# Eight column blocks of an input projection as seven-product units in a two-layer decoder trunk

## The chip, the cores and the metric

The kernel runs on one core of one Trainium2 chip. The metric is the device time of one execution in microseconds. The engines are named as in the profile: PE (TensorE, matrix multiplications), PEld (its weight loads), DVE (VectorE), ACT (ScalarE), POOL (GpSimd) and SP (SyncE, which here only issues loads and stores). Each engine works through its instructions in the order in which they stand in the compiled program, and waits where an instruction needs a result of another engine.

## What is computed

Two identical layers over 512 positions of width 1024, all in 32-bit floats. In each layer four token mixers share one input projection `w_in`, and the branches are gated, projected up, added and projected out; a SwiGLU follows:

```python
def mixer_block(h, cos, sin, w_in, ...):
    u = h @ w_in                       # h = rms_norm(x, ln1)
    (fq, fk, fv, ff, gq, gk, gv, glr, gr, rq, rk, rv, rg, z, xbc, dt, gates) = split_cols(u, IN_SPLITS)
    y_a = forgetting_attention(...)    # fox: softmax over fq, fk, fv with forget gates ff
    y_b = gated linear attention       # gla: gq, gk, gv, glr; its output is gated by silu(gr)
    y_c = retention                    # ret: rq, rk, rv with rotary positions; gated by silu(rg)
    xbc = silu(causal_depthwise_conv(xbc, conv_w, conv_b))
    y_d = ssd_chunked(...)             # ssd: xbc and dt; gated by silu(z)
    g = sigmoid(gates)                 # 4 branches x 1024 columns
    merged = sum over b of g[b] * (y_b @ w_up_b)
    return merged @ w_out
x = x + mixer_block(rms_norm(x, ln1)); x = x + swiglu(rms_norm(x, ln2))
```

The conv has four taps over 768 channels (six tiles of 128). z has 512 columns, gq and gk 256 each.

## The kernel before, in words

**Layout.** Activations stand with features on the 128 partitions and the 512 positions along the row, so a width of 1024 is eight tiles (`KD = 8`). Weights are the stationary operand, in blocks of 128 x 128; eight blocks in the order of use make a slab of 512 KB, which SP loads (L250, tile `wr`).

**Precision.** A 32-bit number is split in a high part that PE takes at its faster 32-bit rate and a rest: `split` (L211) is a cast on ACT (L212) and a subtraction on DVE (L213). A product of two split numbers is three matmuls (`mm3`, L200: high x high, high x low, low x high), all issued by `mm` (L198). So each slab costs ACT a cast of 128x1024 (`wh`) and DVE a subtraction of 128x1024 (`wl`), two slabs ahead of their use (`ahead`, `AHEAD = 2`). The activations are split as well: `xh` is x times the norm's gain, cast on ACT, and `xl` the rest on DVE (`feed`, L392 to 397); the norm's factor per position is multiplied in after the projection, since it is only known later (`rstd`).

**Projections.** `group` (L426) takes four column blocks with the eight tiles of x in the outer loop, so that PE can begin with the first tile; PE needs a slab of weights for every two tiles. `proj` (L435) takes one block of 128 columns: 24 matmuls of 512 columns. A layer begins with a group of four blocks of the conv's input (C_X), two more by `proj`, then the four blocks of z; the conv of tile i (L476: one multiplication and three multiply-adds on DVE, a silu on ACT) is issued beside them. In layer 0 the positions' sines follow (`rotary`, L352), then the wide projection (gv, glr, dt and the forget gates).

**Mixers and fill.** `ssd`, `gla`, `ret` and `fox` are generators that yield between their steps; `drain` (L462) pulls work off a list `fill` at every yield, by its estimated microseconds. The fill holds the projections that are not needed yet (gq, gk, gr, rg, rq, rk, rv, fq, fk, fv), the gates (`gate_quad(b, q)`, L1146: four projections and one sigmoid over 128x2048) and the up-projections (`up_of(b, q)`: four columns blocks, multiplied by the gates and added to `merged`). The compiler's scheduler then orders each engine's instructions by its own estimate of when they can run, so the source does not show the final order alone; the orders in this document are the compiled ones.

**Fox.** For each of four heads and four blocks of 128 queries: scores by two matmuls; an addition of the forget sums on DVE (L1063), the causal mask on POOL (L1064), the row maximum on DVE (L1066), the exponential with its row sum on ACT (`act`, L236), its reciprocal and a scaling on DVE (L1069, L1070). PE transposes the result (L1079), it is split (ACT cast, DVE subtraction), and PE multiplies it with the values. `finish` (L1094, L1095) adds the two halves of a head's output and splits the tile; only then can `up_of(0, .)` use it. After fox the fill still holds the second four gates of branch 0, `mix(gate_quad(0, 1), up_of(0, 0))`, and `up_of(0, 1)`.

**Tables of ACT.** Silu and sine, exponential and logarithm, and sigmoid lie in three sets of functions; `act` (L227) issues a table load (L231) where the set changes. Copies and casts do not ask for one.

**Seven products.** The FFN's first projection already runs most of its column blocks by a scheme of Strassen's kind: a unit of four column blocks by eight row blocks is seen as two by two quarters, each of four row blocks and two column blocks, and the positions are halved to 256. Seven products of quarter sums replace eight. Of the activations, four sums of halves are needed (t1 to t4, made once by `sums`: scaled copies of x on ACT, subtractions on DVE, and a split). Of the weights, the quarters are loaded apart (tiles `rq`, and one `wr`), added and subtracted on DVE and split; three low parts are made by a negated copy on ACT and a load on POOL's queue that adds the weights to it. Results are added from three PSUM banks with copies on ACT (128x256) and additions on DVE.

**Order and buffers.** `wp` holds two raw slabs `wr` and three each of `wh` and `wl`. The mixers' scratch is a pool of 33 tiles of 128x512 (`tp`) and two of 128x2048 for gates (`gp`).

## Time and profile before

| | |
|---|---|
| median of three runs | 1717.66 us (1717.35 to 1718.27) |
| the profiled execution | 1718.72 us, its span 1717.0 us |
| granted clock of TensorE, mean | 0.999 |
| PE busy | 1705.9 us, 10140 matmuls |
| ACT table loads | 40 in one group of the trace, 1.28 us each |
| bytes moved by DMA | 195 MB, 114 GB/s |

Views used in the prediction: the *page* with the share of each engine and, in its rows of 40 slices, PEclk, the clock granted to TensorE in tenths (9 is 90% or more); the *waits* of an engine (what it waited for, the total in us, how often, the longest); the *chain* of work that ended last, in order of time (start, duration, engine, line and count of a piece); the *timeline* (start, duration, engine, line, operation, output <- input, partitions x elements, and in brackets the idle time before it and what ended that); *windows* (a stretch, its length, then busy time and number of instructions of PE, PEld, DVE, ACT and POOL, the granted clock, the busy share of the DMA engines, GB/s); and *groups* of like instructions (count | busy us, mean ns of one | idle time before). A row with x2 covers two instructions. Neighbours on an engine overlap a little in their records, so that the distance of two starts is the better price of one.

### The profile page before, as it was taken

What the parts mean: (1) busy time and instruction counts of PE and PEld (TensorE: products, weight loads), DVE (VectorE), ACT (ScalarE), POOL (GpSimd) and SP (SyncE); (2) the same over time, 40 slices, a digit from 0 to 9 for tenths busy, and PEclk for the clock granted to TensorE, in tenths of its full rate; (3) what the DMA queues carried; (4) which work ended last, traced back from release to release, by engine and by line L of the source; (5) the groups of instructions that cost most, each with busy time, mean ns of one, the idle gap of its engine ahead of it and who ended that gap; (6) DMA issues with size and microseconds to landing.
All of it is one profiled execution on the core that took longest, in us unless ns stands there. A gap on an engine that the chain in (4) does not pass through costs nothing.

```text
span 1717.0 us, 25146 instructions
## 1 busy us (share of the span) xinstructions
PE 1705.9 (99%) x10140; PEld 1484.7 (86%) x10140; DVE 1213.2 (71%) x1683; ACT 861.9 (50%) x1190; POOL 225.2 (13%) x227
## 2 busy tenths in 40 slices
PE   8999999999999999999999999999999999999998
PEld 7878888888888999998988788888888889999998
DVE  5867666768677677675777666767776677767666
ACT  5424543546447646464544254435553574655543
POOL 2032110022101010101010322200221010101010
PEclk9999999999999999999999999999999999999999
DMA  5322222222235657575333222222222365665653
GB/s 199 106 74 74 75 82 78 86 86 74 78 112 143 196 134 186 135 186 121 89 99 115 68 74 75 85 76 89 83 86 82 103 172 161 152 175 139 183 108 102
DMA packets 54693, 195.00 MB, mean 114 GB/s; under 512 B 6064, under 2 KB 6448, under 8 KB 54576
## 3 DMA queue, kind: packets, MB, share of 16 engines
q1 hardware_dynamic: 45072, 160.45, 29.2%
q0 software_dynamic: 8640, 31.46, 10.3%
q8 instruction: 79, 1.29, 0.3%
q10 hardware_dynamic: 864, 1.48, 0.2%
q14 instruction: 38, 0.31, 0.1%
HBM read 191.27 MB, written 2.10 MB: 113 GB/s over the span
## 4 chain that ended last, share of the span: by engine, by line
PE 97%; DVE 1%; DMA 1%; ACT 1%; issue 0%; ACTq 0%; DVEq 0%
PE mm L198 65%; PE mx L198 31%; PE mx L1079 0%; DMA x<-in_x_dram 0%; DMA t<-in_ext_dram 0%; ACT wh L212 0%; DVE wl L213 0%; PE mx L679 0%; DVE t L369 0%; ACT L231 0%; DVE t L836 0%; ACT g L236 0%; DVE t L1168 0%; DVE n L407 0%; PE mx L871 0%
## 5 line engine op out<-in xcount | busy, mean ns | idle before, releaser
L212 ACT CAST wh<-wr 128x1024 fp32r<-128x1024 f32 (+1 forms) x240 | 250.0, 1043 | 378.4 <-PE mm L198 238.0
L198 PE MATMUL mm<-xh,wh 128*128 128x512 f32 (+1 forms) x1184 | 429.2, 362 | 0.9 <-DVE t L1168 0.9
L198 PE MATMUL mm<-xh,wl 128*128 128x512 f32 (+1 forms) x1184 | 428.6, 362 | 0.0
L198 PE MATMUL mm<-xl,wh 128*128 128x512 f32 (+1 forms) x1184 | 427.4, 361 | 0.0
L213 DVE TENSOR_TENSOR wl<-wr,wh 128x1024 fp32r<-128x1024 f32 (+1 forms) x220 | 281.8, 1282 | 119.9 <-ACT wh L212 117.6
L198 PEld LDWEIGHTS mm<-xh,wh 128*128 128x128 f32 x1184 | 222.6, 188 | 35.2 <-DVE t L1168 1.8
L198 PEld LDWEIGHTS mm<-xh,wl 128*128 128x128 f32 x1184 | 222.6, 188 | 35.1 <-issue 1.5
L198 PEld LDWEIGHTS mm<-xl,wh 128*128 128x128 f32 x1184 | 222.6, 188 | 33.7 <-issue 1.1
L198 PE MATMUL mm<-t,wh 128*128 128x512 f32 x448 | 140.3, 392 | 0.0
L198 PE MATMUL mx<-xh,wh 128*128 128x256 f32 (+1 forms) x448 | 136.2, 311 | 3.0 <-ACT wh L212 3.0
L198 PE MATMUL mx<-xl,wh 128*128 128x256 f32 (+1 forms) x448 | 138.5, 309 | 0.0
L1287 POOL DMA_DIRECT2D wl<-in_wsq_dram x60 | 51.9, 864 | 518.0 <-ACT wl L1286 337.1
L198 PE MATMUL mx<-f,wh 128*128 128x512 f32 x352 | 108.3, 390 | 0.0
L198 PE MATMUL mm<-f,wh 128*128 128x512 f32 x352 | 106.0, 390 | 0.0
L198 PEld LDWEIGHTS mm<-t,wh 128*128 128x128 f32 x448 | 83.3, 188 | 17.1
L213 DVE TENSOR_TENSOR l<-rq,wh 128x1024 fp32r<-128x1024 f32 x60 | 73.2, 1219 | 33.1 <-ACT wh L212 18.7
L198 PEld LDWEIGHTS mx<-xh,wh 128*128 128x128 f32 x448 | 84.1, 188 | 9.2 <-ACT wh L212 4.0
L198 PE MATMUL mx<-xh,wl 128*128 128x256 f32 (+1 forms) x288 | 91.0, 327 | 0.0
L198 PEld LDWEIGHTS mx<-xl,wh 128*128 128x128 f32 x448 | 84.2, 188 | 5.1
L198 PE MATMUL mm<-t,wl 128*128 128x512 f32 x224 | 87.5, 390 | 0.0
L212 ACT CAST wh<-rq 128x1024 fp32r<-128x1024 f32 x60 | 62.9, 1049 | 43.9 <-PE mm L198 21.5
L198 PEld LDWEIGHTS mm<-f,wh 128*128 128x128 f32 x352 | 66.1, 188 | 13.5
(275 smaller groups left out, 3457.2 us busy)
## 6 DMA issues: line engine op xcount, KB each, us to landing
wr<-in_wst_dram SPq DMA_DIRECT2D x216, 512.0 KB, 3.5
rq<-in_wsq_dram SPq DMA_DIRECT2D x60, 512.0 KB, 5.3
wl<-in_wsq_dram POOLq DMA_DIRECT2D x60, 512.0 KB, 7.1
wr<-in_wsq_dram SPq DMA_DIRECT2D x20, 512.0 KB, 7.3
out_dram<-x SPq DMA_DIRECT2D x8, 256.0 KB, 2.0
x<-in_x_dram SPq DMA_DIRECT2D x3, 512.0 KB, 7.2
wr<-in_wst_dram SPq DMA_DIRECT2D x4, 256.0 KB, 5.6
x<-in_x_dram SPq DMA_DIRECT2D x2, 256.0 KB, 4.5
```

Of the source, the lines that this page charges most:

```text
L198: T.matmul(o, lhsT=l, rhs=r, start=start, stop=stop, skip_group_check=True)
L212: A.copy(out=hi, in_=src)
L213: V.tensor_tensor(out=lo, in0=src, in1=hi.bitcast(F32), op=ALU.subtract)
L1287: G.dma_start(out=lo, in_=wsq[j], accum_op=ALU.add)
```

## The change

Per layer, eight column blocks of `w_in` leave the plain projections: the four of z, and two each of gq and gk. They become two units of the seven-product scheme, which run directly behind the six plain blocks of the conv's input. For that, `sums` and `strassen` move out of the FFN, with the function that finishes a unit as an argument (the FFN calls them as before), and `sums` becomes a generator: in the layer's first group of four blocks, its four sums are issued one at a time at the tiles k = 4, 5, 6 and 7, and the first two negated copies and accumulating loads at k = 6 and 7. At k = 4 in layer 0 the squares and the constants' loads are issued first, as before.

The conv of all six tiles, and in layer 0 `rotary`, move behind the products. One pool `kp` of eight tiles of 128x1024 takes the conv's input, the products' results, the gates and the merged sum; the 128x2048 gate tiles go, and `tp` shrinks from 33 tiles to 24. A sigmoid now covers a pair of gate blocks (128x1024), and a silu of gr and rg one block. The fill is put in another order: `gate_quad(3, 0)` and rv move ahead of ssd, rg behind it, fq and fk into gla, and `gate_quad(0, 1)` into fox; behind fox only `up_of(0, 0)` and `up_of(0, 1)` are left. The table of slabs with wide blocks (`TOKEN`) and the counts of slabs follow. In the changed kernel `mm` is L203, `split` L217 and L218, `act` L241 and its table load L236, fox's transposes L1293.

The diff, cut to what matters:

```diff
-TOKEN = (10, 11, 12, 25, 26, 41, 42)
+TOKEN = (6, 7, 8, 15, 16, 33, 34)
...
-    def mixers():
-        return phase(gp=2, vp=2, bd=1, tp=33)
+    def front():
+        outer = phase(g=64, kp=8)
+        return outer, phase(tq=1, ep=4, rp=5, gl=192, lp=2)
...
-            if hook and k == 4:
-                hook()
+            if hook and k in hook:
+                hook[k]()
...
+    def sums(tb, g, FT):
+        xg = []
+        def scaled(ks):
+            for k in ks:
+                t = FT([P, 2, S])
+                for i in range(2):
+                    act(out=t[:, i], in_=x[:, k + i], func=AF.Copy, scale=g[:, k + i:k + i + 1])
+                xg.append(t)
+        scaled((0, 2))
+        one_, two = slice(0, H), slice(H, S)
+        def make(n, f):
+            t = FT([P, HK, H])
+            for i in range(2):
+                a, b = f(i)
+                V.tensor_tensor(out=t[:, 2 * i:2 * i + 2], in0=a, in1=b, op=ALU.subtract)
+            split(t, *tb[n])
+            return t
+        t1 = make("t1", lambda i: (xg[i][:, :, two], xg[i][:, :, one_]))
+        yield
+        scaled((4, 6))
+        t2 = make("t2", lambda i: (xg[2 + i][:, :, two], t1[:, 2 * i:2 * i + 2]))
+        yield
+        make("t3", lambda i: (xg[2 + i][:, :, two], xg[i][:, :, two]))
+        yield
+        make("t4", lambda i: (xg[2 + i][:, :, one_], t2[:, 2 * i:2 * i + 2]))
...
+        cols = [(C_Z, C_Z + 2 * P), (C_GQ, C_GK)]
+        begin, run = strassen("w_in", l, [tuple(pairs_of(c) for c in u) for u in cols], tb1, KT, True, front_done)
+        steps = sums(tb1, PR("ln1"), KT)
         def first():
-            for k in range(KD):
-                n1.square(k)
-            constants()
-        ps4 = group("w_in", l, [C_X + P * i for i in range(4)], n1, KD, first if l == 0 else None)
+            if l == 0:
+                for k in range(KD):
+                    n1.square(k)
+                constants()
+            next(steps)
+        def third():
+            next(steps)
+            begin(-1)
+        def fourth():
+            next(steps, None)
+            begin(-2)
+        ps4 = group("w_in", l, [C_X + P * i for i in range(4)], n1, KD, {4: first, 5: lambda: next(steps), 6: third, 7: fourth})
         n1.rstd(True)
...
+        run()
+        scope.close()
+        scope = phase(vp=2, bd=1, tp=24)
...
         for i in (4, 5, 0, 1, 2, 3):
-            cin[i] = scaled(ps4[i] if i < 4 else proj("w_in", l, C_X + P * i, n1, KD))
-        conv(4, cin[4])
-        conv(5, cin[5])
-        for i in range(4):
-            sz[i] = scaled(proj("w_in", l, C_Z + P * i, n1, KD))
-            act(out=sz[i], in_=sz[i], func=AF.Silu)
             conv(i, cin[i])
...
-                    if i == 0:
-                        st["t"] = gp.tile([P, 4, S], F32, tag="g", name=nm("g"))
+                    if i % 2 == 0:
+                        st["t"] = KT([P, 2, S])
...
-                    if i == 3:
+                    if i % 2:
                         act(out=st["t"], in_=st["t"], func=AF.Sigmoid)
...
-        fill += [keep(gq, j, C_GQ + P * j, 0.125) for j in range(2)] + [keep(gk, j, C_GK + P * j) for j in range(2)]
-        fill += silus([C_GR, C_GR + P, C_RG, C_RG + P])
+        fill += gate_quad(3, 0) + silus("gr", C_GR, pair_tiles) + tokmajor(rv, C_RV)
         fill += [keep(rq, j, C_RQ + P * j) for j in range(2)] + [keep(rk, j, C_RK + P * j) for j in range(2)]
+        if l == 0:
+            rotary()
         drain(ssd(), PACE[0])
...
-        fill += mix(gate_quad(2, 0), up_of(1, 1)) + mix(gate_quad(2, 1), up_of(2, 0)) + mix(gate_quad(0, 0), up_of(2, 1))
+        fill += mix(gate_quad(2, 0), up_of(1, 1)) + mix(gate_quad(2, 1), up_of(2, 0)) + mix(gate_quad(0, 0), up_of(2, 1)) + gate_quad(0, 1)
         drain(fox(), PACE[3])
-        fill += mix(gate_quad(0, 1), up_of(0, 0)) + up_of(0, 1)
+        fill += up_of(0, 0) + up_of(0, 1)
```

The products of one layer stand in PE's order as (unit, product): (0,1) (0,2) (0,6) (0,5) (0,7) (1,1) (0,3) (0,4) (1,6) (1,5) (1,7) (1,2) (1,3) (1,4). The number of matmuls rises by 4 x (168 - 96) = 288, the number of table loads in ACT's order from 41 to 88.

More of the change, by code (lines that the diff above doesn't have):

```diff
@@ L490, in scaled @@
             return t
[L492 to L506 removed]
+        tb1 = rights(n1, True)
@@ new lines, in layer, with pairs_of, front_done @@
+        cin, gq, gk = [None] * 6, [None] * 2, [None] * 2
+        gates = {}
+        def pairs_of(c):
+            return c, c + P
+        def front_done(u, a, b):
+            both(a, 0.125 if u else None)
+            both(b)
+            if u == 0:
+                for i, t in enumerate((a, b)):
+                    act(out=t, in_=t, func=AF.Silu)
+                    sz[2 * i:2 * i + 2] = t[:, 0], t[:, 1]
+            else:
+                gq[:] = a[:, 0], a[:, 1]
+                gk[:] = b[:, 0], b[:, 1]
@@ L1390, in ready_for @@
         def ready_for(n):
-            m = PLAIN if n == 0 else sum(PARTS[:n])
-            return strassen(list(range(m, sum(PARTS[:n + 1]), 2)))
+            f0 = PLAIN if n == 0 else sum(PARTS[:n])
+            units = [(pairs_of(f * P), pairs_of(FFN + f * P)) for f in range(f0, sum(PARTS[:n + 1]), 2)]
+            return strassen("w_ffn_in", l, units, tb2, FT, False, lambda u, a, b: swiglu(a, b))
         nn = None
@@ L1397, in hook @@
         def hook():
-            sums()
+            for _ in sums(tb2, PR("ln2"), FT):
+                pass
             begin(-2)
-        ps4 = group("w_ffn_in", l, [0, FFN, P, FFN + P], n2, KD, hook)
+        ps4 = group("w_ffn_in", l, [0, FFN, P, FFN + P], n2, KD, {4: hook})
         n2.rstd()
@@ L1413, in layer @@
             end = part == len(PARTS) - 1
-            cap[0] = len(keys) // SLAB + n + (FRONT // SLAB if end and not last else 0)
+            cap[0] = len(keys) // SLAB + n + (6 if end and not last else 0)
             run()
```

380 lines of the change are left out of this document (188 added, 192 removed).

## The prediction

> **What bounds the kernel now.** I read the page first: the engines' shares, then the chain that ended last, then the waits of PE, then timelines of the places that the change touches.
>
> ```profile
> PE 1705.9 (99%) x10140; PEld 1484.7 (86%) x10140; DVE 1213.2 (71%) x1683; ACT 861.9 (50%) x1190; POOL 225.2 (13%) x227
> PE 97%; DVE 1%; DMA 1%; ACT 1%; issue 0%; ACTq 0%; DVEq 0%
> PE mx L198 <- ACT wh L212: 3.0, 3, 1.6
> PE mm L198 <- POOL t L325: 1.4, 1, 1.4
> PE mx L198 <- DVE t L213: 1.2, 2, 0.7
> PE mm L198 <- DVE t L1168: 0.9, 2, 0.5
> PEclk9999999999999999999999999999999999999999
> ```
>
> PE is 97% of the chain and waits 6.5 us in all (the four lines of waits: total, times, longest), at full clock in every slice. So PE work that is removed is time, and so is each new wait of PE: it works in order, and nothing absorbs a gap. Pace, from the chain:
>
> ```profile
> 505.30 21.76 PE mm L198 x96
> 650.71 8.16 PE mm L198 x72
> 860.39 21.77 PE mx L198 x96
> ```
>
> 96 matmuls of N=512 take 21.76 us (0.2267 each; the third row is layer 1's first group), 72 of N=256 inside the FFN's seven products 8.16 us (0.1133 each): products already run without a gap there.
>
> **Part 1, the products.** A unit of four column blocks is 4 x 8 x 3 = 96 matmuls of 0.2267 = 21.76 us before, and 7 x 2 x 4 x 3 = 168 of 0.1133 = 19.04 us after. Four units: 4 x 2.72 = **-10.9 us**, all on the path. A unit loads the same bytes as four slabs did, and three accumulating loads of 512 KB on POOL's queue besides. I price them at nothing:
>
> ```profile
> 26.00:32.00 6.00, 6.00 (x28) 4.98 (x27) 3.06 (x3) 2.11 (x2) 0.00 (x0) 1.00 0.48 172
> ```
>
> Even in the start-up the DMA engines are busy 0.48 of the time by then (the last but one number), and in SP's order the five new loads stand behind those of the first three slabs. If that cover were gone, the fourth slab would come late by what part 2 allows at its upper end.
>
> **Part 2, the start.** ACT is the engine that PE waits for there, and it is nearly gapless:
>
> ```profile
> 13.04 1.12 ACT L212 CAST wh<-wr 128x512 fp32r<-128x512 f32 x2
> 14.56 1.34 ACT L236 ACTIVATE xh<-x,pr 128x512 fp32r<-128x512 f32 x2 [0.40 <-DMA x<-in_x_dram]
> 15.80 1.14 ACT L236 ACTIVATE n<-x 128x512 f32<-128x512 f32 x2
> 16.84 1.32 ACT L236 ACTIVATE xh<-x,pr 128x512 fp32r<-128x512 f32 x2
> 18.90 0.63 ACT L236 ACTIVATE n<-x 128x512 f32<-128x512 f32 x1 [0.73 <-DVE n L407]
> 19.44 1.03 ACT L212 CAST wh<-wr 128x1024 fp32r<-128x1024 f32 x1
> 20.52 0.51 PE L198 MATMUL mx<-xh,wh 128*128 128x512 f32 x1 [1.05 <-ACT wh L212]
> ```
>
> The third slab's cast ends at 20.47 and PE starts on it at 20.52. ACT's order at this place, before (the cast of the third slab is wh_194) and after (wh_207; k_ are scaled copies of x, t1h the split of the first sum):
>
> ```order
> L212 CAST wh_146<-wr_109 128x512 x2
> L236 ACTIVATE xh_134<-x,pr 128x512 x2
> L236 ACTIVATE n_232<-x 128x512
> L236 ACTIVATE n_235<-x 128x512
> L236 ACTIVATE xh_134<-x,pr 128x512 x2
> L236 ACTIVATE n_238<-x 128x512
> L212 CAST wh_194<-wr_114 128x1024
> ```
>
> Up to that cast stood casts and squares alone. After:
>
> ```order
> L241 ACTIVATE k_270<-x,pr 128x512 x2
> L217 CAST wh_153<-wr_115 128x512 x2
> L241 ACTIVATE xh_141<-x,pr 128x512 x2
> L241 ACTIVATE n_245<-x 128x512
> L241 ACTIVATE k_296<-x,pr 128x512 x2
> L241 ACTIVATE n_248<-x 128x512
> L217 CAST t1h_171<-k_273 128x1024
> L241 ACTIVATE xh_141<-x,pr 128x512 x2
> L241 ACTIVATE k_299<-x,pr 128x512 x2
> L217 CAST wh_207<-wr_120 128x1024
> ```
>
> Six k_ copies of these rows and two earlier ones now stand ahead of that cast: 8 x 0.62 (two xh in 1.24, 14.56 to 15.80) + 0.95 for t1h = 5.9 us; one square less (0.5) and the idle 0.40 + 0.73 give some back. **+4.0 us** (3 to 6, the upper end without what is given back).
>
> **Part 3, the entry of layer 1.** The sums add 8 subtractions of 0.6 and 4 of 1.14 (9.4 us) to DVE, under the six plain blocks:
>
> ```profile
> 853.00:876.00 23.00, 23.00 (x103) 19.08 (x102) 22.72 (x30) 15.01 (x21) 5.42 (x3) 1.00 0.32 92
> 854.08 0.68 DVE L1424 TENSOR_TENSOR x<-x,f 128x512 f32<-128x512 f32 x1
> 855.87 1.22 DVE L213 TENSOR_TENSOR wl<-wr,wh 128x1024 fp32r<-128x1024 f32 x1
> 874.51 1.21 DVE L213 TENSOR_TENSOR wl<-wr,wh 128x1024 fp32r<-128x1024 f32 x1
> ```
>
> (The first row's fourth pair is DVE: 22.72 of 23 us; starts of following rows lie 0.6 and 1.14 apart.) DVE came free at 875.7, PE's group of four ends at 882.16 (860.39 + 21.77); by 875.7 + 9.4 = 885.1 it would be done, which makes the fifth slab's subtraction 1 to 3 us late. **+2.0** (0 to 4).
>
> **Part 4, conv.** It lay under the four z projections, which are gone:
>
> ```profile
> L480 DVE SCALAR_TENSOR_TENSOR t<-t,pr,t 128x510 f32<-128x510 f32 x6 | 4.5, 744 | 0.0
> L477 DVE TENSOR_SCALAR t<-t,pr 128x512 f32<-128x512 f32 x6 | 3.1, 537 | 0.0
> ```
>
> 3.1 + 3 x 4.5 = 16.6 us of DVE a layer (three such rows, one for each tap) now stand behind the products, with weight splits queued between them; in layer 0 rotary comes on top. Walking the order with these durations, one weight split is 1 us late and the SSD's first sums another 1.5, less in layer 1. **+2.5** in all (0 to 6). The state's memset, which now stands behind the products on POOL, is needed only in the GLA: nothing. That gates, merged sum and the products' results share eight tiles makes writers wait for older readers, but those readers stand far ahead in the order: nothing, and if not, rival D.
>
> **Part 5, the end of fox.** Here is the largest term. Before, the last softmax and its product ran under projections of the last gates:
>
> ```profile
> 442.54 0.73 DVE L1063 SCALAR_TENSOR_TENSOR t<-mx,cq,t 128x512 f32<-128x512 f32 x1
> 443.95 0.28 POOL L1064 TENSOR_SCALAR_AFFINE_SELECT t<-t 128x128 f32<-128x128 f32 x1
> 444.26 2.33 DVE L213 TENSOR_TENSOR wl<-wr,wh 128x1024 fp32r<-128x1024 f32 x1
> 446.51 0.67 DVE L1066 TENSOR_REDUCE fmx<-t 128x1 f32<-128x512 f32 x1
> 447.21 0.72 ACT L236 ACTIVATE t<-t,fmx 128x512 f32<-128x512 f32 x1 [2.14 <-DVE fmx L1066]
> 448.05 1.28 ACT L231 ACT_TABLE_LOAD   x1
> 450.30 1.91 ACT L236 ACTIVATE g<-g 128x2048 f32<-128x2048 f32 x1
> 448.26 0.49 DVE L1070 TENSOR_SCALAR t<-t,frs 128x512 f32<-128x512 f32 x1
> 452.87 0.97 ACT L212 CAST t<-mx 128x512 fp32r<-128x512 f32 x2 [0.66 <-PE mx L1079]
> 453.49 0.69 DVE L213 TENSOR_TENSOR t<-mx,t 128x512 fp32r<-128x512 f32 x1 [1.83 <-ACT t L212]
> 453.05 4.79 PE mm L198 x21
> 459.70 0.58 ACT L1094 COPY t<-mx 64x512 f32<-64x512 f32 x1 [3.43 <-PE mx L198]
> 460.31 0.68 DVE L1095 TENSOR_TENSOR t<-mx,t 64x512 f32<-64x512 f32 x1 [2.79 <-ACT t L1094]
> 461.03 0.62 ACT L212 CAST t<-t 128x512 fp32r<-128x512 f32 x1 [0.75 <-DVE t L1095]
> 459.66 10.51 PE mm L198 x46
> ```
>
> PE had 4.79 us of projections behind the last transposes and 10.51 us behind the last product. On PE, before (mx_4044 and mx_4067 take the last transposes, mm_4087 is a projection for the gates):
>
> ```order
> L1079 MATMUL mx_4044<-cs,t_3920 128x128
> L1079 MATMUL mx_4044<-cs,t_3989 128x128
> L1079 MATMUL mx_4067<-cs,t_3989 128x128 x2
> L198 MATMUL mm_4087<-xh_134,wl_4020 128x512
> L198 MATMUL mm_4087<-xh_134,wh_4019 128x512
> L198 MATMUL mm_4087<-xl_135,wh_4019 128x512
> ```
>
> The projection goes on behind them. On PE after, at the same place (mx_4504 transposes, mx_4397 the output, mm_4523 the first up-projection of this same output):
>
> ```order
> L1293 MATMUL mx_4504<-cs,t_4446 128x128 x2
> L203 MATMUL mx_4397<-t_4496,t_2796 128x256
> L203 MATMUL mx_4397<-t_4497,t_2796 128x256
> L203 MATMUL mx_4397<-t_4496,t_2799 128x256
> L203 MATMUL mx_4397<-t_4497,t_2799 128x256
> L203 MATMUL mx_4397<-t_4508,t_2802 128x256
> L203 MATMUL mx_4397<-t_4509,t_2802 128x256
> L203 MATMUL mx_4397<-t_4508,t_2805 128x128
> L203 MATMUL mx_4397<-t_4509,t_2805 128x128
> L203 MATMUL mm_4523<-t_4519,wh_4460 128x512
> ```
>
> No projection is left between them. And on ACT, after (t_4446 the last softmax, k_4410 the last pair of gates):
>
> ```order
> L241 ACTIVATE t_4446,frs_4453<-t_4446,fmx_4451 128x512
> L236 ACT_TABLE_LOAD
> L241 ACTIVATE k_4410<-k_4410 128x1024
> L236 ACT_TABLE_LOAD
> L217 CAST t_4496<-mx_4491 128x512
> L217 CAST t_4508<-mx_4504 128x384
> ```
>
> The cast that the output's product waits for stands behind a sigmoid and two table loads, as gates are now taken in pairs. Price in layer 0: exponential to cast is 1.28 + about 1.05 (an estimate: half of 1.91 and a little, for half the columns) + 1.28 + 0.5 (half of the cast pair's 0.97) = 4.1 us; scale and transposes take 2.1 of it beside, so PE waits 2.0. The second split (two subtractions, 0.6 apart) against PE's own work: 0.8. Then copy, add and cast, from 459.70 to 461.03 + 0.62: 2.0, and 0.2 until the copy starts. The last score itself comes 2 late: ACT and DVE are behind from the pair before it, and 20 matmuls (4.5 us) cover a chain of 0.73 + 0.28 (select on POOL) + 0.67 + 0.84 (447.21 to 448.05) + 0.2 + 0.49 = 3.2 that two weight splits of 1.14 are queued among. Sum 7. In layer 1 the order leaves 3 matmuls instead of 8 ahead of those transposes, so 9; one earlier step there, where five copies queue behind a table pair, another 2. **+18** (8, if only the finishing chains and the table pairs show; 24, if weight splits in that chain take 2.33 us, as one did here at 444.26, and not 1.2).
>
> The Trainium skill ("ScalarE: Activation LUTs", section "What ACT_TABLE_LOAD costs") gives 186 ns + 0.833 ns an element for an activation with immediates, so 1.04 us for 128x1024, which no row here shows; by it the sum stays as it is.
>
> **Sum.** -10.9 + 4.0 + 2.0 + 2.5 + 18 = +15.6 on the profiled execution, 1718.72 (span 1717.0 and 1.7 around it), which lies 1.06 above the median 1717.66: 1717.7 + 15.6 = **1733 us**.
>
> **Rivals.** *A, faster:* ACT runs ahead at the end of fox, the gates' pairs are done before the last score, and PE meets finished casts: then the start's 4 us and little else is lost, -10.9 + 4 + 2 = -5, 1713. For it: ACT is only 50% busy. Against: the table loads rise from 41 to 88 in the order, 47 x 1.28 = 60 us more of ACT, and the sequence above is fixed. It decides if less than 5 us of part 5 appear. Chance 0.11. *B, no change:* only the finishing chains (2 x 2.2) and some 4 us of part 5 show beside parts 2 and 3: -10.9 + 4 + 2 + 4.4 + 4 = +3.5 at most, 1715 to 1721; 0.12. *C, the clock:* PE would be mostly idle for 6 to 9 us at two places, and the granted clock could fall behind them. At half the clock for 4 us, about as long as the larger single gaps, each place costs 2 us more: 1737. This trace has no wait longer than 1.6 us and a clock of 1.00 throughout, so it neither shows nor excludes it; 0.12. The Trainium skill ("TensorE: Matmul & The Clock Gate", section "HAM oscillation — how this bites in real kernels") states it so: no idle gap over about 3.4 us, or the array goes back to half its clock. *D, more of the same:* the 47 added table loads also reach PE in the mixers' other steps (8 us, some six loads), 1741; 0.10. My forecast: 0.55.
>
> About 0.2%, 3.4 us, is what a measurement can tell from no change. Faster: A, 0.11. Same: B, 0.12. Slower: the forecast, C and D, 0.77. The range runs from the lower ends (3 + 0 + 0 + 8 - 10.9 = 0, 1718), which leaves out A and half of B, to D with some of the upper ends, 1745.
>
> **What would show it.** The waits of PE should rise from 6.5 to about 33 us, most of them on casts and subtractions of t (L217, L218) at two places, between 460 and 500 us and some 850 us later; PE should start its third slab near 24.5. The FFN's parts should keep their length. If PE's waits stay under 15 us, part 5 is wrong; if a unit of products takes over 20 us, part 1 is.

## The result, and the profile after

| | before | after |
|---|---|---|
| median | 1717.69 us (4 runs) | **1769.72 us** (4 runs, 1767.71 to 1772.70) |
| profiled execution, its span | 1718.72, 1717.0 us | 1772.70, 1770.8 us |
| granted clock, mean | 0.999 | 0.985 |

The ratio is 1.0304 (95%: 1.0286 to 1.0322): 52 us slower. The sign was forecast; the size, +52 against +15.6, lies outside the range. The profiled execution is the slowest of the four and has the lowest clock (0.985; the others 0.987 and 0.988), so that what is counted in its trace is a little more than what the median lost.

The page after: busy shares of the engines, shares of the chain that ended last, the granted clock in 40 slices, and the group of table loads.

```profile
PE 1726.9 (98%) x10428; PEld 1503.6 (85%) x10428; DVE 1250.3 (71%) x1739; ACT 972.5 (55%) x1329; POOL 244.5 (14%) x239
PE 85%; DVE 6%; ACT 5%; issue 3%; DMA 1%; POOL 0%; ACTq 0%; POOLq 0%
PEclk9999999999989999999999999999999899999999
L236 ACT ACT_TABLE_LOAD x80 | 102.6, 1283 | 1.3
```

PE's part of the chain fell from 97% to 85%. Its busy time rose by 21 us, although the change takes work from it: some matmuls are slower. Two slices show a clock below 0.9, and a slice is 44 us. The waits of PE, the largest (total us, times, longest us):

```profile
PE mx L203 <- ACT t L217: 12.1, 5, 3.1
PE mx L203 <- ACT wh L217: 5.4, 5, 2.6
PE mm L203 <- DVE k L1370: 4.4, 4, 1.5
PE mm L203 <- ACT t L217: 4.1, 2, 2.1
```

All waits together are 38.6 us, against 6.5 before. That is 32 more and explains neither +52 nor, with the products' 10.9 taken off, the 63 lost. To see where it goes, two stretches of 20 us of before:

```profile
340.00:360.00 20.00, 20.00 (x94) 16.56 (x93) 15.48 (x26) 11.95 (x16) 4.90 (x5) 1.00 0.34 106
480.00:500.00 20.00, 20.00 (x90) 16.58 (x89) 13.82 (x19) 9.13 (x11) 0.00 (x0) 1.00 0.34 106
```

And the places that lose most after (first pair PE, then PEld, DVE, ACT, POOL, the granted clock):

```profile
340.00:360.00 20.00, 15.23 (x62) 11.36 (x60) 13.97 (x19) 13.27 (x18) 0.00 (x0) 0.97 0.29 90
360.00:380.00 20.00, 18.83 (x70) 14.06 (x70) 17.95 (x29) 14.05 (x20) 5.32 (x4) 0.86 0.09 34
480.00:500.00 20.00, 15.46 (x65) 12.36 (x64) 9.42 (x17) 9.31 (x13) 0.41 (x2) 0.80 0.17 52
900.00:920.00 20.00, 16.70 (x65) 13.02 (x64) 16.32 (x21) 11.45 (x15) 3.01 (x3) 0.83 0.62 172
1220.00:1240.00 20.00, 15.10 (x53) 10.10 (x52) 15.53 (x22) 14.55 (x22) 0.27 (x1) 0.90 0.24 79
1360.00:1380.00 20.00, 13.30 (x56) 10.49 (x55) 10.17 (x17) 10.08 (x15) 1.45 (x2) 0.73 0.16 52
```

Before, PE filled such stretches at clock 1.00. After, 13 to 19 us of 20, at a mean clock down to 0.73. The ends of fox (480, 1360) and the entry of layer 1 (900) were forecast. The first two rows and the fifth, where ret hands over to fox (below: the joint), were not.

A balance adds this up. For each stretch of 20 us I take its length less what the matmuls begun in it take at full pace (0.2267 us for 512 columns, in proportion for fewer, at least 0.057), and subtract the same for the stage in before. "At half pace" is half the time that matmuls took inside stretches of clock 0.50; it is part of the column before it.

| place | forecast | measured, us over before | of that at half pace |
|---|---|---|---|
| products | -10.9 | -10.9 | |
| start, 0 to 60 | +4.0 | +9.2 | 3.6 |
| entry of layer 1, 880 to 960 | +2.0 | +8.7 | 3.2 |
| conv | +2.5 | about 0 | |
| joint of ret and fox, layer 0, 340 to 400 | - | +10.2 | 3.2 |
| the same, layer 1, 1220 to 1260 | - | +9.7 | 2.9 |
| end of fox, layer 0, 480 to 520 | +18 with the next row | +8.7 | 3.6 |
| end of fox, layer 1, and the step before it, 1320 to 1400 | | +14.2 | 3.9 |
| all else | - | +3 | |
| sum | +15.6 | +52.7 (span: +53.8) | 20.4 |

**What half pace is.** PE's timeline at the start, third slab:

```profile
24.43 0.80 PE L203 MATMUL mx<-xh,wh 128*128 128x512 f32 x1 [2.63 <-ACT wh L217]
25.02 0.63 PE L203 MATMUL mx<-xl,wh 128*128 128x512 f32 x1
25.45 0.63 PE L203 MATMUL mx<-xh,wh 128*128 128x512 f32 x1
...
29.32 0.39 PE L203 MATMUL mx<-xh,wl 128*128 128x512 f32 x1
29.55 0.39 PE L203 MATMUL mx<-xh,wh 128*128 128x512 f32 x1
```

And the granted clock (third number from the end) in two half microseconds there:

```profile
24.50:25.00 0.50, 0.50 (x1) 0.43 (x2) 0.50 (x2) 0.50 (x2) 0.00 (x0) 0.50 0.00 0
...
28.00:28.50 0.50, 0.50 (x4) 0.41 (x3) 0.50 (x2) 0.50 (x2) 0.50 (x1) 1.00 0.36 57
```

At the end of a wait of 2.63 us the clock drops to 0.50, at 24.39; starts lie 0.43 us apart instead of 0.23, until 27.81. Seven such drops stand in this trace: at 24.39, 41.46, 358.9, 492.0, 911.9, 1236.1 and 1369.2, for 3.4, 3.4, 6.8, 10.2, 6.8, 6.8 and 13.7 us. All lengths are multiples of 3.41 us, and the drops lie on one grid of that period through the whole execution.

What decides is how much matmul work falls into a period of that grid. Take, for each period, the time that its matmuls need (as in the balance, twice that at clock 0.50) as a share of 3.41 us. Over the traces of all 17 kernels here, a period at full clock with a share below 0.35 was followed by one at half clock in 72 of 74 cases, between 0.35 and 0.45 in 7 of 26, above that in 2 of 8416. Back to full came behind a share of at least 0.8 in 77 of 80 cases, between 0.5 and 0.8 in 4 of 34, below that in none of 34. The profile's own busy time of PE runs higher than this share: the period before 41.46 shows PE busy for 2.67 of 3.41 us and no wait over 0.53 us, but its matmuls, eight of them with a single column, come to a share of 0.48 (it is one of the two exceptions above 0.45). Into the period ahead of each of the other six drops falls a wait of 2.3 to 3.1 us. So a wait of little more than 2 us that falls badly on the grid is enough, and a period at half pace costs up to 1.7 us more. The Trainium skill ("TensorE: Matmul & The Clock Gate", section "Part 1: The HAM clock gate (the "warmup" mystery)") has a free-running window of 3413 ns and two states, 4/8 and 8/8; these traces agree. Its section "HAM oscillation — how this bites in real kernels", from which the prediction took a limit of about 3.4 us for a gap, is too lenient here: no wait ahead of these seven drops was longer than 3.1 us.

**The joint.** PE's timeline where ret ends in layer 0 (`mx<-t,cr` are the eight matmuls that sum fox's squares for the norm):

```profile
353.49 0.73 PE L203 MATMUL mm<-t,wh 128*128 128x512 f32 x2 [1.47 <-DVE k L1370]
358.21 0.50 PE L203 MATMUL mx<-t,cr 128*128 128x512 f32 x1 [3.07 <-ACT t L217]
358.94 4.34 PE L203 MATMUL mx<-t,cr 128*128 128x512 f32 x7 [0.22 <-DVE t L218]
```

PE first waits for a gate's multiplication on DVE (L1370), then for the cast of fox's squares. The other seven norm matmuls then start 0.6 us apart, at clock 0.50, with no projection between them. In before, projections of the fill stand between the eight in six places. After, none does.

**The end of fox**, from the chain of after (start, duration, piece):

```profile
488.18 1.28 ACT L236
489.48 0.71 ACT k L241
490.55 1.28 ACT L236
491.85 0.59 ACT t L217
492.46 0.70 DVE t L218
493.21 1.77 PE mx L203 x7
495.00 0.59 ACT t L1308
...
496.33 0.63 ACT t L217
497.00 6.83 PE mm L203 x18
```

This is the sequence of part 5 piece by piece: table load, sigmoid, table load, cast, subtraction, product, copy, addition, cast, with PE idle for 2.35 us ahead of the product and for 2.04 us behind it. The chain counts 0.71 us of the sigmoid and the rest of it as issue; in ACT's timeline it takes 1.06 us, and part 5 had estimated 1.05. The trace of before had the size already, in the FFN: 22 activations of 128x1024 on L236 at 1.06 us. The 18 matmuls at the end take 6.83 us where full pace is 4.08.

### The profile page after: what moved, and what is told of

Its sections match the earlier page's. It is cut to its first block, busy times and chain, and to the rows that moved or that the text cites. A ratio compares the mean times of both kernels' runs of the same rounds, so it can differ in the third digit from the quotient of the medians.

```text
span 1770.8 us, 25962 instructions
## 1 busy us (share of the span) xinstructions
PE 1726.9 (98%) x10428; PEld 1503.6 (85%) x10428; DVE 1250.3 (71%) x1739; ACT 972.5 (55%) x1329; POOL 244.5 (14%) x239
## 3 DMA queue, kind: packets, MB, share of 16 engines
q0 software_dynamic: 10368, 37.75, 12.1%
## 4 chain that ended last, share of the span: by engine, by line
PE 85%; DVE 6%; ACT 5%; issue 3%; DMA 1%; POOL 0%; ACTq 0%; POOLq 0%
PE mm L203 55%; PE mx L203 29%; DVE wl L218 1%; ACT L236 1%; ACT wh L217 1%; ACT t L241 1%; ACT k L241 1%; ACT t L217 0%; DVE xl L399 0%; DMA wl<-in_wsq_dram 0%; DVE x L1481 0%; PE mx L1293 0%; DVE f L1480 0%; DVE rq L513 0%; ACT xh L241 0%
## 5 line engine op out<-in xcount | busy, mean ns | idle before, releaser
L217 ACT CAST wh<-wr 128x1024 fp32r<-128x1024 f32 (+1 forms) x228 | 237.2, 1041 | 309.4 <-PE mm L203 159.6
L203 PE MATMUL mm<-xh,wh 128*128 128x512 f32 (+1 forms) x1088 | 389.7, 358 | 1.7 <-DVE k L1370 1.4
L203 PE MATMUL mm<-xh,wl 128*128 128x512 f32 (+1 forms) x1088 | 389.2, 358 | 1.1 <-DVE wl L218 1.1
L203 PE MATMUL mm<-xl,wh 128*128 128x512 f32 (+1 forms) x1088 | 388.3, 357 | 0.0
L218 DVE TENSOR_TENSOR wl<-wr,wh 128x1024 fp32r<-128x1024 f32 (+1 forms) x204 | 254.6, 1249 | 100.5 <-ACT wh L217 98.9
L203 PEld LDWEIGHTS mm<-xh,wh 128*128 128x128 f32 x1088 | 206.4, 190 | 32.2 <-DVE k L1370 1.3
L203 PEld LDWEIGHTS mm<-xh,wl 128*128 128x128 f32 x1088 | 205.8, 189 | 32.4 <-DVE wl L218 2.0
L203 PEld LDWEIGHTS mm<-xl,wh 128*128 128x128 f32 x1088 | 206.3, 190 | 29.3 <-issue 0.5
L203 PE MATMUL mx<-xh,wh 128*128 128x256 f32 (+1 forms) x512 | 154.3, 310 | 6.0 <-ACT wh L217 5.0
L203 PE MATMUL mx<-xl,wh 128*128 128x256 f32 (+1 forms) x512 | 157.5, 308 | 0.0
L203 PE MATMUL mm<-t,wh 128*128 128x512 f32 x448 | 146.8, 405 | 9.2 <-ACT t L217 4.1
L218 DVE TENSOR_TENSOR l<-rq,wh 128x1024 fp32r<-128x1024 f32 x72 | 87.9, 1221 | 40.7 <-ACT wh L217 24.8
L203 PEld LDWEIGHTS mm<-t,wh 128*128 128x128 f32 x448 | 85.1, 193 | 29.2 <-ACT t L217 4.5
L203 PE MATMUL mx<-f,wh 128*128 128x512 f32 x352 | 108.2, 390 | 0.0
L203 PEld LDWEIGHTS mx<-xh,wh 128*128 128x128 f32 x512 | 97.2, 190 | 12.6 <-ACT wh L217 6.1
L203 PE MATMUL mm<-f,wh 128*128 128x512 f32 x352 | 105.9, 389 | 0.0
L217 ACT CAST wh<-rq 128x1024 fp32r<-128x1024 f32 x72 | 75.5, 1048 | 51.2 <-PE mm L203 22.4
L203 PEld LDWEIGHTS mx<-xl,wh 128*128 128x128 f32 x512 | 97.3, 190 | 5.4
L203 PE MATMUL mx<-xh,wl 128*128 128x256 f32 (+1 forms) x304 | 95.4, 325 | 0.8 <-DVE wl L218 0.4
L203 PE MATMUL mm<-t,wl 128*128 128x512 f32 x224 | 89.7, 400 | 0.0
```

The source lines that it names most:

```text
L203: T.matmul(o, lhsT=l, rhs=r, start=start, stop=stop, skip_group_check=True)
L217: A.copy(out=hi, in_=src)
L218: V.tensor_tensor(out=lo, in0=src, in1=hi.bitcast(F32), op=ALU.subtract)
```

## The experiments

The theory after the result: of the eight projections a layer that become products, four (gq and gk) had stood in the fill, and without them PE is left bare at the joints and at the end of fox; short waits there also halve the clock. Rivals: the doubled table loads; the order of the fill alone; waits alone, with no price of the clock. Each kernel's time stands beside the kernel before on the same chip (medians 1717.86 to 1718.35).

**1. The last gates back behind fox.**

```diff
-        fill += ... + mix(gate_quad(0, 0), up_of(2, 1)) + gate_quad(0, 1)
+        fill += ... + mix(gate_quad(0, 0), up_of(2, 1))
         drain(fox(), PACE[3])
-        fill += up_of(0, 0) + up_of(0, 1)
+        fill += mix(gate_quad(0, 1), up_of(0, 0)) + up_of(0, 1)
```

> Only the last four gates of branch 0 go back behind fox, as in the kernel before. Cover and clock (my theory: what was lost are projections that stood beside serial chains; PE waits there, and for some us behind each wait it runs at half pace): the places at the two ends of fox, about 9.5 and 13 us more than before, go; 1770 - 22 = 1748 us (1743 to 1753), PE's waits at these two places under 2 us, no half clock there; the places near 355, 915 and 1235 us stay. Tables (rival: the added table loads of ACT make the chains late whatever PE has to do beside): the chains are as late as now, at most 6 us come back, 1764 or more.

Measured: 1765.26 us (1.0274, 1.0259 to 1.0290), 4.5 under after, not 22. PE's timeline at the end of fox, layer 0:

```profile
484.56 0.76 PE L1293 MATMUL mx<-cs,t 128*128 128x128 f32 x5 [1.57 <-DVE t L1284]
...
491.20 2.08 PE L203 MATMUL mm<-t,wh 128*128 128x512 f32 x4 [2.04 <-ACT t L217]
```

Bare as before the edit: the fill within fox ran dry three steps earlier, and the compiler moved most of the four gates up into the hole (the last 18 of their 96 matmuls stand behind the wait, from 495.2 on). That the place of these gates was the fault does not hold. That the amount is short is the reading left; runs 4 to 6 test it.

**2. Two sigmoids of a quad back to back**, which brings the table loads from 80 to 52 in the group:

```diff
-                    if i % 2:
-                        act(out=st["t"], in_=st["t"], func=AF.Sigmoid)
+                    if i == 3:
+                        for t in gates[b][-2:]:
+                            act(out=t, in_=t, func=AF.Sigmoid)
```

> The gates stay in pairs of 128x1024, but the two sigmoids of four gates are issued behind each other, so that the table is changed once for four gates as before and not twice: up to 32 table loads of 1.28 us fewer. Tables: 10 us or more come back, 1760 or less. Cover and clock: the chains still have no work of PE beside them; under 5 us, 1765 to 1772.

Measured: 1759.42 (1.0241, 1.0225 to 1.0256), the rival's number: the pairs cost 10 us here.

**3. Pairs in the kernel before**, the same alone:

```diff
-                    if i == 3:
-                        act(out=st["t"], in_=st["t"], func=AF.Sigmoid)
+                    if i % 2:
+                        act(out=st["t"][:, i - 1:i + 1], in_=st["t"][:, i - 1:i + 1], func=AF.Sigmoid)
```

> The kernel before with the sigmoid of a quad of gates taken in two pairs: 16 more table loads in the order (57 for 41), nothing else changed. Tables: 16 x 1.28 us of ACT and later casts, 5 us or more, 1723 and up. Cover: PE has projections beside all of it, under 3 us, 1717 to 1721.

Measured: 1717.36 (0.9997, 0.9988 to 1.0006). The groups of before and of this kernel:

```profile
L231 ACT ACT_TABLE_LOAD x40 | 51.3, 1283 | 0.7
```

```profile
L231 ACT ACT_TABLE_LOAD x56 | 71.8, 1283 | 0.9
```

Sixteen more loads, 20.5 us of ACT, cost nothing where PE has projections to run meanwhile. So the 10 us of run 2 look like a price of bare places, not of the loads as such; the two runs differ in the number of loads too, 28 and 16.

**4. The fill alone, in the kernel before:** gq and gk as plain projections behind z, the fill in the order of after, and no products.

```diff
             conv(i, cin[i])
+        gq = [scaled(proj("w_in", l, C_GQ + P * j, n1, KD), 0.125) for j in range(2)]
+        gk = [scaled(proj("w_in", l, C_GK + P * j, n1, KD)) for j in range(2)]
...
-        fill += [keep(gq, j, ...)] + [keep(gk, j, ...)]
-        fill += silus([C_GR, C_GR + P, C_RG, C_RG + P])
+        fill += gate_quad(3, 0) + silus([C_GR, C_GR + P], "r") + tokmajor(rv, C_RV)
...
-        fill += ... + mix(gate_quad(0, 0), up_of(2, 1))
+        fill += ... + mix(gate_quad(0, 0), up_of(2, 1)) + gate_quad(0, 1)
```

> The kernel before with the fill of the changed one and nothing else of it: the four projections of gq and gk leave the fill and run plainly behind z, the fill stands in the changed kernel's order, behind fox only the up-projections of branch 0 are left. No products, no sums, sigmoids over four gates. Cover: the ends of fox stand bare as in the changed kernel, 10 to 13 us each with the half pace behind them: 1718 + 23 = 1741 (1735 to 1750). Tables, or the sums: 1718 to 1725.

Measured: 1752.20 (1.0195, 1.0178 to 1.0212): +34.3 with not one seven-product unit in the front. PE's waits show the same places:

```profile
PE mm L198 <- DVE t L1169: 14.4, 4, 7.0
PE mm L198 <- ACT t L212: 4.1, 2, 2.0
```

The first row is the joints, 7.0 us in one piece; the second the end of fox, 2.0 us in each layer, as in run 1. This is the largest part of the loss, and it is neither the products nor the shared tiles, which this kernel does not have.

**5. and 6. Its two halves.** Run 5 has only the first edit of run 4 (gq and gk leave the fill, order of before). Run 6 has only the other two, with gq and gk kept in the fill.

> The kernel before with only gq and gk taken out of the fill and run plainly behind z; order of the rest, the four gates behind fox and the pace as before. Amount (what costs is that four projections a layer are no longer there to be put beside the chains; the fill runs dry in ssd already and 28.6 us of it, by its own estimates, are left when fox starts, for 49.4 before): 1718 + 25 to 35 = 1743 to 1753, as with the whole of the changed fill. Order: 1718 to 1726.

> The kernel before with only the order of the fill changed as in the changed kernel (four gates of branch 3 and rv ahead of ssd, fq and fk in the GLA's list, the last four gates in fox); gq and gk stay at its head, so that 49.4 us are left at the start of fox as before. Amount: 1716 to 1723. Order: 1735 or more.

Measured: 1805.01 (1.0503, 1.0487 to 1.0519) and 1732.67 (1.0085, 1.0070 to 1.0100). PE's largest row of waits in run 5 (the row of 14.4 us of run 4 stands there too, unchanged):

```profile
PE mx L198 <- ACT t L212: 22.4, 8, 6.4
```

Neither theory's number holds: the amount alone costs 87 us, far over its 1753, and the order alone 14, which it had at nothing (7.4 and 7.1 of that at the GLA, 240 and 1100 us). But run 6 decides where the loss of run 4 comes from. With gq and gk in the fill and the same new order, PE's longest wait is 1.4 us:

```profile
PE mx L198 <- ACT t L212: 2.9, 2, 1.4
```

The balance, without subtracting before, counts some 3 us at each joint and 1 at each end of fox, as in before. In run 4 it counts 12.6 and 12.1 us at the joints, 7.5 and 8.4 at the ends of fox. So both are bare because gq and gk are missing from the fill. Order and amount also depend on each other: gq and gk are 42 us of PE work in the two layers by the program's estimates, and when they go, ssd and gla run dry as well unless the fill is put in another order. The new order answers that, saves 52 us (86.7 - 34.3), and cannot make good the rest.

**7. fq and fk back into the fill of ret**, and `up_of(3, 1)` into gla in their place:

```diff
-        fill += [keep(fq, j, ...)] + [keep(fk, j, ...)]
+        fill += up_of(3, 1)
         drain(gla(), PACE[1])
+        fill += [keep(fq, j, ...)] + [keep(fk, j, ...)]
```

> Only fq and fk go back into ret's fill, as before, and two up-projections of branch 3 take their place in the GLA's; the eight matmuls of fox's norms, which stood in a row in the order, have projections between them again. Cover: the places near 355 and 1235 us (10.5 each over before) lose most of it, the ends of fox keep theirs; 1770 - 14 = 1756 (1750 to 1762). Rival (the waits there come from the tables and from DVE's queue, not from the order): 1765 or more.

Measured: 1749.86 (1.0184, 1.0169 to 1.0199), 20 us under after, 6 better than expected. What the balance counts at the joints went from 12.7 and 12.0 to some 7.5 each; most of the rest of the gain, 6 us, lies at the end of fox in layer 1, and some 4 at the start and the entry, where nothing was edited. So which projections are left at the joints matters beside how many. What the last 7 us at each are (DVE's queue, from which gate and up-multiplications come late) stays open.

**8. Fill that lasts to the end of fox:** run 1 with fox's `PACE` at 6.0 instead of 7.5, so that less is taken from the fill at each step.

> The last four gates of branch 0 behind fox, and the pace of fox lowered from 7.5 to 6.0 us of fill a step, so that the fill lasts to the end of fox: in the order 24 projection matmuls now stand behind the last transposes and some 20 behind the last score, as before. Cover (what is lost at the end of fox is that four projections a layer, gq and gk, left the fill): the two ends of fox cost nothing over before, 1770 - 21 = 1749 us (1744 to 1755), and no half clock there. Rival (the chains there are longer than before, by table loads and shared tiles, whatever PE does): 1760 or more.

Measured: 1759.25 (1.0236, 1.0220 to 1.0251), 6 better than run 1, 10 short of the expected. The waits at the ends of fox are gone (none over 0.2 us is left), but the middle of fox, where the balance counted about 1 us, now has 5.3 and 5.7 (at 420 and 1280). Fill can be moved, and the hole moves along.

**9. and 10. The sums late.** The four sums and the first loads that accumulate are issued behind the layer's first group instead of in it; to hold the compiler to it, the gain is touched behind the last tile of x. In run 9 it is copied to a new tile of 32 bytes a partition; in run 10 it is rewritten in place (the diff).

```diff
-        ps4 = group(..., {4: first, 5: lambda: next(steps), 6: third, 7: fourth})
+        ps4 = group(..., {4: first} if l == 0 else None)
+        g1 = PR("ln1")
+        V.scalar_tensor_tensor(out=g1, in0=n1.hi[:, KD - 1, :KD].bitcast(F32), scalar=0.0, in1=g1, op0=ALU.mult, op1=ALU.add)
         n1.rstd(True)
+        for _ in range(4):
+            next(steps, None)
+        begin(-1)
+        begin(-2)
```

> The four sums and the first two accumulating loads are issued behind the first group, and the scaled copies are made to depend on the last tile of x, so that no sum stands ahead of the casts of the first slabs. Cover and clock: the start (9 us over before) and the entry of layer 1 (9 us) lose most of it, PE starts its third slab near 20.5 us and no half clock stands at 24 or 41 us; 1770 - 10 = 1760 (1754 to 1766). Rival: the sums then come late for the products that need them, and the wait only moves behind the six plain blocks; 1768 or more.

> The late sums once more, with the gain changed in place by nothing (a zero times the last tile of x is added) and no new tile, so that all buffers lie as in the changed kernel; the matmuls of 256 columns should run at 0.113 us again and not at 0.119. The start and the entry of layer 1 (9 us each over before) lose most of it: 1770 - 11 = 1759 (1754 to 1765). Rival: what the earlier kernel with late sums lost was the late sums, 1775 or more.

Measured: 1788.05 (1.0410, 1.0393 to 1.0427) and 1764.18 (1.0268, 1.0252 to 1.0283). The same piece of the FFN in the chain of after, and of run 9:

```profile
570.26 2.05 PE mm L203 x18
```

```profile
570.56 2.14 PE mm L203 x18
```

In this piece a matmul of 256 columns takes 0.119 us instead of 0.114. Over the whole of run 9, matmuls of 256 columns start 0.118 us apart and those of 512 columns 0.231, in run 10 0.114 and 0.228: some 27 us in all. So run 9 says little about the sums. Run 10 does. PE's third slab:

```profile
20.84 0.50 PE L203 MATMUL mx<-xh,wh 128*128 128x512 f32 x1 [0.35 <-ACT wh L217]
```

It begins at 20.84, as before the change (20.52), and not at 24.43. The start's loss fell from 9.2 to 3.0, the entry's from 8.7 to about 4. By the medians the whole gained only 5.5 us and not 10; the profiled executions lie 10.2 apart, but they are the slowest of four after and the fastest of four here. How much of the two places the median lost is open between these numbers.

**11. Idle matmuls.** 36 matmuls a layer on constants, whose results nobody reads: 12 at the start of fox, 24 in its last steps. They cost 72 x 0.2267 = 16.3 us where PE has no room for them.

> Adds 36 matmuls a layer on constants, whose results nobody reads: 12 at the start of fox and 24 at its end, in the order just ahead of the places where PE waits. Cover and clock: PE waits no shorter for the chains, but the half pace behind the waits at these four places (11 stretches of 3.4 us at half clock in the changed kernel, about 14 us of lost work) mostly goes; 1770 - 10 = 1760 (1755 to 1765). Waits only (rival: the half pace costs nothing of its own): the added matmuls cost nothing to 5 us, 1770 to 1776.

Measured: 1769.07 (1.0296, 1.0281 to 1.0312). Where the clock was 0.50 from 492.0 on, it now is 1.00 and PE busy:

```profile
492.00:496.00 4.00, 3.84 (x24) 3.21 (x22) 1.16 (x2) 1.09 (x3) 0.00 (x0) 1.00 0.00 0
```

Half pace fell from 20.4 to 9.3 us (the first 13 us left out) and waits from 38.6 to 28.7; the dummies' own 16.3 us took most of that back. The time lies just under the rival's 1770 to 1776 and cannot tell the two apart.

**12. and 13. The clock by itself**, in the kernel before. Ahead of each of the last four column blocks of the FFN's second projection at the end, the activations wait for a chain of DVE instructions on the previous block's result. Run 13 has 13 unread matmuls in each such gap besides (the lines with `pd`; run 12 lacks them).

```diff
+                    g = NT()
+                    V.tensor_copy(out=g, in_=prev)
+                    for _ in range(4):
+                        V.tensor_scalar(out=g, in0=g, scalar1=1.0, scalar2=None, op0=ALU.mult)
+                    pd = MX()
+                    for _ in range(13):
+                        mm(pd, R("uo")[:, P:], acts[0][0], True, True)
+                    h = acts[0][0][:, :KD]
+                    V.scalar_tensor_tensor(out=h, in0=g[:, :KD], scalar=0.0, in1=h.bitcast(F32), op0=ALU.mult, op1=ALU.add)
```

> The kernel before, with four waits put into its last 11 us: ahead of each of the last four column blocks of the second FFN projection (12 matmuls, 2.72 us each) PE waits for a chain on DVE of a copy out of PSUM, four copies and a touch of one operand, some 0.7 + 4 x 0.55 + 0.3 = 3.2 us. Nothing else of PE can run there. Clock (a gap of this length halves PE's pace for a stretch behind it): 1718 + 4 x 3.2 + some 8 to 11 for blocks at half pace = 1740 (1737 to 1743). Waits only: 1731 (1729 to 1733).

> The same four chains, and in each gap 13 matmuls of 512 columns whose results nobody reads (13 x 0.2267 = 2.95 us). Clock: the gaps stay, the half pace goes: 1731 (1729 to 1734), 8 us or so under the bare gaps. Waits only: as the bare gaps, or a little longer.

Measured: 1745.25 (1.0157, 1.0142 to 1.0172) and 1738.69 (1.0120, 1.0105 to 1.0135). The same stretch, bare and filled, and the first matmuls behind one of its gaps:

```profile
1704.00:1731.00 27.00, 15.09 (x36) 10.80 (x36) 11.13 (x25) 0.00 (x0) 0.00 (x0) 0.68 0.10 39
1706.44 1.22 PE L198 MATMUL mm<-f,wh 128*128 128x512 f32 x2 [5.54 <-DVE f L1448]
```

```profile
1704.00:1731.00 27.00, 21.48 (x83) 16.13 (x83) 14.48 (x32) 0.00 (x0) 0.00 (x0) 0.94 0.16 59
1716.29 0.73 PE L198 MATMUL mm<-f,wh 128*128 128x512 f32 x2 [0.95 <-DVE f L1451]
```

DVE's chain is as long in both, 3.2 to 3.3 us from its copy to the touch. What differs is the pace of the useful blocks: from PE's start to the first reading of the result the four take 5.5, 4.4, 5.3 and 5.5 us bare, and 4.6, 3.1, 3.1 and 3.1 filled, 6.9 us less, beside 6.6 between the medians. The bare kernel has the clock at 0.50 behind all four gaps, the filled one only behind the first, where PE still waited 2.58 us. So the clock has a price of its own beside the waits, shown. Both runs came 5 and 8 us above expectation, as the gaps were longer than meant.

**14. and 15. All repairs together:** runs 2, 7, 8 and 10 in one kernel, with fox's `PACE` at 6.0 and at 6.7.

> Late sums, sigmoids in fours, fq and fk in ret, and the fill of fox stretched to its end, together. If the places are independent: 1770 - 11 - 21 - 14 - 4 (what is left of the fours' 10, since much of it lies at the same places) = 1720 (1712 to 1728), beside 1718 before. If one cause stands behind several of them (too little fill in the whole mixer): the cover only moves and 1735 or more is left.

> All four mendings, with fox at 6.7 us of fill a step and not at 6.0. At 6.0 the middle of fox lost 4.5 us a layer over before, since its steps were covered too thinly; at 6.7 the fill runs out some three steps earlier. Amount: what the middle gains the end loses, 1736 (1732 to 1742). If the middle is a matter of one bad place in the order: 1728 or less.

Measured: 1736.57 (1.0110, 1.0093 to 1.0127) and 1732.13 (1.0078, 1.0061 to 1.0095). The gains do not add: singly they were 10.3, 19.9, 10.5 and 5.5 us, 46, and together 33; the waits that they remove are partly the same ones. At 6.0 half pace is down to some 5 us (the first 13 us left out). The waits left at 6.7:

```profile
PE mm L203 <- DVE t L1383: 7.5, 4, 1.9
PE mm L203 <- ACT t L217: 4.1, 2, 2.0
```

The first are up-projections multiplied by their gates at the joints, the second again the end of fox. No version of the changed kernel beat the kernel before.

## Why the prediction was right and wrong

**Part 1, the products: right.** The chain of after has

```profile
64.00 5.44 PE mm L203 x48
```

5.44 / 48 = 0.1133 us each, as priced, so the units take 19.04 us and gain 10.9; the accumulating loads and the FFN cost nothing that shows.

**Part 2, the start: mechanism right, size off.** The third slab starts at 24.43, forecast "near 24.5", and ACT's copies and `t1h` are the cause (run 10). Of the 9.2 us lost, 5.6 are waits, inside the step's 3 to 6, and 3.6 half pace, at 24.39 and at 41.46; the step had the wait and not what follows from it.

**Part 3, the entry of layer 1: direction right, size off.** +8.7 instead of +2.0, 3.2 of it half pace:

```profile
905.76 1.05 ACT L217 CAST t2h<-k 128x1024 fp32r<-128x1024 f32 x1 [2.46 <-DVE k L476]
...
909.55 0.61 ACT L217 CAST n<-n 128x512 fp32r<-128x512 f32 x1
910.22 0.50 PE L203 MATMUL mm<-n,cr 128*128 128x512 f32 x1 [2.73 <-ACT n L217]
```

I had asked when DVE could deliver the fifth slab. The larger wait, 2.73 us, is on ACT: the cast of the norm's sum of squares ends at 910.2, behind the casts of t2, t3 and t4 (1.04 us each) and of a slab, and the first of these had itself waited 2.46 us for DVE. Late sums halved the loss (run 10).

**Part 4, conv: wrong by its 2.5 us.** Nothing to be seen there.

**Part 5, the end of fox: right in place and sequence, wrong in its cause, and it missed the joints.** Without half pace, the ends of fox and the step before the second one lost 8.7 - 3.6 + 14.2 - 3.9 = 15.4 us against 18. In layer 0 PE waits 2.35 us for the cast, where the step had 2.0, and 2.04 for the finishing chain, where it had 2.2. What failed is where the step took the loss from. It read that the last softmax and its product had run "under projections of the last gates", and so looked for bare chains only at the place those gates were moved from. Run 1 put them back and the end of fox stayed bare. What covers a chain is what the fill still holds, and I had not added it up: by the program's own estimates 49.4 us of the earlier lists are left when fox begins before, and 28.6 after, since gq and gk (four projections, 20.8 us a layer) left it. Pulling the last four gates into fox, another 20.8, makes that good within fox and takes it from behind it. The same sum would have pointed at the joints, which the prediction has at nothing and where 13.8 us were lost without half pace; run 6, with gq and gk in the fill, has neither loss. The eight norm matmuls without a projection between them stood in the compiled order too, some hundred rows from the place that the step walks through.

**Rival C, the clock, was true beside the forecast and mis-sized.** I gave it two places at 2 us; it was seven drops and 20.4 us. I had taken gaps of 3 to 4 us as the condition, and 2 us were enough; and a place at half pace loses up to 3.9 us, because the clock mostly comes back only behind a period with a share of work of at least 0.8 (77 of 80), which a place full of waits doesn't offer. By the balance, without half pace, the forecast's parts come to -10.9 + 5.6 + 5.5 + 0 + 15.4 = 15.6, its own sum. That is luck, as start and entry lost 5.1 more and conv and the end of fox 5.1 less than forecast. The joints bring 13.8, half pace 20.4 and all else 3, together 52.8. That PE's waits come to 38.6 us, near the "about 33" of the prediction, is luck as well: some 13 of them stand at the joints, where none were forecast.

**Rival D, the added table loads, holds in part.** Run 2 gives 10 us for the pairs, near D's 8, but in a kernel that lacks cover; run 3, in one that has it, gives nothing. **A and B are out:** 38.6 us of waits where under 15 would have spoken for them.

Summed the other way: products -10.9, the fill alone +34.3 (run 4), pairs +10.3 (run 2), and start and entry 17.9 from the balance are +51.6, against 52.0. That the two meet so closely is partly luck: run 10 got back only 5.5 of the 17.9 by the medians, and in run 14 the gains overlapped (46 and 33). The fill is the largest part either way. Whether a version with more scratch tiles, in which projections could be kept longer, would gain the 10.9 us was not tried; the change itself took nine tiles from that pool (33 to 24).

## What to carry to other kernels

Work that waits in a list to cover serial chains is worth more than its own time: before it is made cheaper and moved to the front, add up what the list still holds at the start of each later stage, and compare it with those stages' chains. Look for bare chains in the whole compiled order, not only where the source was edited. And price a wait of 2 us or more of PE twice: once for itself, and once for matmuls at half pace behind it.

## What the runs showed of the hardware that was not expected

- The granted clock has two values in these traces, 1.00 and 0.50, on a grid of 3.41 us, and falls behind a period with less than about 0.35 to 0.45 of matmul work (72 of 74 below 0.35), not only behind idle ones.
- A new tile of 32 bytes a partition made matmuls of 256 columns 3% slower (0.114 to 0.118 us, mean) and those of 512 columns 1% (0.228 to 0.231), and the kernel 24 us: run 9 against run 10, otherwise the same edit. That it shifts the addresses of the tiles behind it is my guess; it wasn't tested.
- Sixteen more table loads, 1.28 us each, changed nothing measurable in a kernel whose PE was covered (0.9997, 0.9988 to 1.0006).
